# Groups of matmuls added behind the last product of a two-layer decoder trunk

## The chip, the cores and the metric

The kernel runs on one core of a Trainium2 chip. The metric is the device time of one execution in microseconds (us), lower is better; for the kernel before it is the median of two runs. A core has five engines with a queue each: TensorE (PE in the profile, with its weight loads shown apart as PEld), VectorE (DVE), ScalarE (ACT), GpSimd (POOL) and SyncE (SP). They wait for each other through semaphores. A matmul takes a stationary operand (the weights, 128 x 128) and a moving operand (128 partitions by up to 512 columns) from SBUF and writes to a bank of PSUM.

## The reference

The kernel computes a decoder trunk of two layers over 512 tokens with a model width of 1024. Cut to what matters:

```python
def hybrid_layer(x, ...):
    h = rmsnorm(x, g_mix)
    z = h @ w_in                       # one projection, split into nine parts
    ya = sliding_window_sink_attention(aq, ak, av, sinks) @ w_a
    r  = chunkwise_retention(rq, rk, rv)
    yb = (group-normed r * silu(rg)) @ w_b
    x = x + (sigmoid(ga) * ya + sigmoid(gb) * yb) @ w_out
    h2 = rmsnorm(x, g_mlp)
    return x + square(relu(h2 @ w_up)) @ w_down

def reference(x, ...):
    for l in range(2):
        x = hybrid_layer(x, ...)
    return rmsnorm(x, g_final)
```

## The kernel before

Activations lie with the width on the partitions: eight tiles of 128 by 512 tokens. Every float32 factor is held as a sum of two reduced parts of type float32r, a high and a low one: `xh` and `xl` for the activations, `hi` and `lo` for a unit of weights (1024 columns). A product is three matmuls, high by high, high by low and low by high, all accumulated in one PSUM bank (function `products`, lines 395 to 397; in `by_halves`, line 410, the same three in another order). Matmuls have 512 moving columns in the plain projections and 256 in those parts that work by halves (`pair`, and `output` with its line 1301).

Weights stream from device memory; ScalarE makes `hi` (line 343), VectorE `lo` (line 344). These tiles have 1024 + 64 columns of room. For the units named in `ASIDE = ("pair", "wo")` the weights begin `LINE = 16` elements into the tile, for all others at its start. In the built program `xh`, `xl` and the tiles `hi` and `lo` all begin at the same remainder modulo 256 bytes (64 elements), as do the tiles of activations, so where weights begin can be told by the elements past that place, modulo 64: 0 or 16 in this kernel.

PSUM has eight banks in two pools, `ps_mm` with five and `ps_aux` with three. A new bank of a pool is the one that was used longest ago, and the framework makes its first matmul wait for whoever used it last. The framework also orders each engine's queue. `tc.issue_after(ins)` fixes an order on one engine: what is issued inside comes after `ins`. `latest[0]` holds the last matmul that was issued.

The program ends with the second layer's last block, `down_plain`: the last product (lines 395 to 397 with `mm<-hi,r`, its final tile in two halves of 256 columns, its stationary operand a tile of activations named `r`, which begins at 0), then on VectorE and ScalarE the last normalisation (lines 1656 to 1685), then two stores of `y_out` (lines 1683 and 1686), then a closing in which SyncE waits for every engine and queue.

Some matmuls in the kernel are issued without their result being read: eight at the start (line 375, `warm`), and one at lines 1289 and 1560 each, which write a bank before others accumulate into it.

Of the kernel before, what the change touches and what calls it, by code (L numbers as in the profile page):

```python
# [17 lines left out]
P = 128  # L18
T = 512
# [61 lines left out]
class Slots:  # L81
# [12 lines left out]
    def one(self):  # L94
        part = [f for f in self.free if 0 < len(f) < 4]
        f = min(part, key=len) if part else next(f for f in self.free if f)
        return f.pop(0)
# [1683 lines left out]
        layer_body(layer)  # L1781

def _by_chunk(w, cols):

    return w[:, cols].reshape(-1, P, len(cols)).transpose(1, 0, 2)
# [158 lines left out]
```

## Time and profile before

| What | us |
|---|---|
| median of 2 runs | 1455.31 (1455.17 to 1455.45) |
| the profiled execution's own time | 1457.31 |
| its span, first to last instruction | 1455.2 |

In the page's rows "busy" is the time in which an engine had an instruction in work; matmuls overlap, so a busy TensorE need not be at its peak. PEclk is the clock that TensorE was granted, in tenths of full speed, for 40 equal slices of the span. The chain that ended last is followed back from the last instruction to what released each step. A row of it has a start, a length and what it was; rows of equal work are merged, with their count behind an x. Timeline rows begin with a start and a duration, too; from the start of one row to the start of the next is the pace, which for matmuls is less than the duration of one.

### The profile page before, as it was taken

Reading aid. Unit: us, or ns where it says so; the run is one execution under the profiler, and the core shown is the slowest. Engines: PE = TensorE matmul, PEld = TensorE weight load, DVE = VectorE, ACT = ScalarE, POOL = GpSimd, SP = SyncE. Lnnn points to the kernel's source line nnn. Section 1 sums busy time; section 2 is a strip of 40 time slices with the busy share of each in tenths; the row PEclk is TensorE's granted clock in tenths of the full one; section 3 lists DMA queues with packets and bytes.
Section 4 is the critical chain, followed back from the end, with each engine's and each line's share of the span. In section 5 each row is a group of like instructions: output and inputs, shape, how many; then the busy total and the mean of one; then the engine's idle time right before and its main releaser. Section 6 shows DMA issues by size and latency. Waiting matters only on the chain.

```text
span 1455.2 us, 22150 instructions
## 1 busy us (share of the span) xinstructions
PE 1443.0 (99%) x8041; PEld 1258.8 (87%) x8041; DVE 1167.0 (80%) x1762; ACT 969.2 (67%) x1592; POOL 222.6 (15%) x329
## 2 busy tenths in 40 slices
PE   9999999999999999999999999999999999999998
PEld 7888888888988999999888888888889799999997
DVE  6978876866998888888778788687778988787885
ACT  6657555543687777777756575565437877777775
POOL 0011012112101111112201110112120011111120
PEclk9999999999999999999999999999999999999999
DMA  7598359799745677666955983797875477777664
GB/s 258 177 290 225 105 165 303 237 247 248 232 124 196 191 200 186 175 182 179 310 177 170 295 222 108 215 293 223 221 214 175 138 202 199 195 193 197 177 188 149
DMA packets 96428, 297.57 MB, mean 204 GB/s; under 512 B 11328, under 2 KB 11456, under 8 KB 90432
## 3 DMA queue, kind: packets, MB, share of 16 engines
q0 software_dynamic: 35936, 125.58, 37.2%
q1 hardware_dynamic: 59664, 169.27, 33.5%
q8 instruction: 63, 1.03, 0.3%
q10 hardware_dynamic: 720, 1.31, 0.2%
q14 instruction: 45, 0.37, 0.1%
HBM read 256.54 MB, written 115.87 MB: 256 GB/s over the span
## 4 chain that ended last, share of the span: by engine, by line
PE 94%; DMA 2%; ACT 2%; DVE 1%; issue 1%; SPq 0%; DVEq 0%; ACTq 0%
PE mm L395 23%; PE mm L396 23%; PE mm L397 22%; PE wo L1301 5%; PE b L395 2%; PE b L396 2%; PE b L397 2%; PE rv L396 2%; PE rv L395 2%; PE rv L397 2%; PE mm L410 2%; DMA raw<-w_pair_in 1%; PE score L778 1%; PE pT L743 1%; PE r L397 1%; PE r L396 1%
## 5 line engine op out<-in xcount | busy, mean ns | idle before, releaser
L343 ACT ACTIVATE hi<-raw 128x1024 fp32r<-128x1024 f32 (+1 forms) x387 | 394.3, 1021 | 257.5 <-PE mm L396 137.1
L344 DVE TENSOR_TENSOR lo<-raw,hi 128x1024 fp32r<-128x1024 f32 (+1 forms) x388 | 452.3, 1173 | 105.8 <-ACT hi L343 104.4
L395 PE MATMUL mm<-xh,hi 128*128 128x512 f32 (+1 forms) x976 | 343.1, 355 | 1.6 <-ACT xh L418 0.9
L396 PE MATMUL mm<-xl,hi 128*128 128x512 f32 (+1 forms) x976 | 343.6, 355 | 0.0
L397 PE MATMUL mm<-xh,lo 128*128 128x512 f32 (+1 forms) x976 | 339.5, 354 | 0.0
L395 PEld LDWEIGHTS mm<-xh,hi 128*128 128x128 f32 x976 | 183.9, 189 | 27.6 <-ACT xh L418 1.6
L396 PEld LDWEIGHTS mm<-xl,hi 128*128 128x128 f32 x976 | 185.0, 190 | 24.2
L397 PEld LDWEIGHTS mm<-xh,lo 128*128 128x128 f32 x976 | 182.7, 188 | 23.6
L397 PE MATMUL mm<-r,lo 128*128 128x256 f32 (+1 forms) x608 | 187.9, 309 | 0.0
L396 PE MATMUL mm<-r,hi 128*128 128x256 f32 (+1 forms) x608 | 187.9, 309 | 0.0
L395 PE MATMUL mm<-r,hi 128*128 128x256 f32 (+1 forms) x608 | 185.6, 309 | 0.5 <-ACT mm L1476 0.5
L395 PEld LDWEIGHTS mm<-r,hi 128*128 128x128 f32 x608 | 114.7, 189 | 8.5 <-ACT mm L1476 0.7
L396 PEld LDWEIGHTS mm<-r,hi 128*128 128x128 f32 x608 | 115.2, 189 | 7.8
L397 PEld LDWEIGHTS mm<-r,lo 128*128 128x128 f32 x608 | 114.1, 188 | 6.2
L1624 POOL DMA_DIRECT2D y<-eu x56 | 62.3, 1351 | 370.8 <-DVE eu L1609 370.2
L396 PE MATMUL mm<-lo,r 128*128 128x512 f32 (+1 forms) x276 | 104.6, 388 | 0.0
L397 PE MATMUL mm<-hi,r 128*128 128x512 f32 (+1 forms) x276 | 101.3, 387 | 0.0
L395 PE MATMUL mm<-hi,r 128*128 128x512 f32 (+1 forms) x276 | 98.4, 390 | 0.9 <-ACT eu L1619 0.6
L395 PE MATMUL b<-hi,r 128*128 128x512 f32 x180 | 70.5, 392 | 1.6 <-DVE eu L1609 1.2
L396 PE MATMUL b<-lo,r 128*128 128x512 f32 x180 | 70.3, 390 | 0.0
L1301 PE MATMUL wo<-r,hi 128*128 128x256 f32 x384 | 68.0, 281 | 0.0
L397 PE MATMUL b<-hi,r 128*128 128x512 f32 x180 | 67.9, 390 | 0.0
(323 smaller groups left out, 2679.5 us busy)
## 6 DMA issues: line engine op xcount, KB each, us to landing
raw<-w_in_in SPq DMA_DIRECT2D x73, 512.0 KB, 5.9
sums_down<-w_down_in POOLq DMA_DIRECT2D x30, 1024.0 KB, 11.6
sums_up<-w_pair_in POOLq DMA_DIRECT2D x56, 512.0 KB, 10.5
raw<-w_down_in SPq DMA_DIRECT2D x45, 512.0 KB, 7.8
raw<-w_pair_in SPq DMA_DIRECT2D x84, 256.0 KB, 3.7
y<-y POOLq DMA_DIRECT2D x63, 256.0 KB, 9.2
y<-eu POOLq DMA_DIRECT2D x61, 256.0 KB, 8.0
raw<-sums_down SPq DMA_DIRECT2D x30, 512.0 KB, 7.3
```

The source lines that it names most:

```text
L343: state["high"] = nc.scalar.activation(hi[:, at], raw[:, at], AF.Copy).ins
L344: nc.vector.tensor_tensor(lo[:, at], raw[:, at], f32(hi[:, at]), ALU.subtract)
L395: nc.tensor.matmul(ps, ah, bh, start=start and i == 0, stop=False, **more)
L396: nc.tensor.matmul(ps, ah, bl, start=False, stop=False, **more)
L397: latest[0] = nc.tensor.matmul(ps, al, bh, start=False, stop=stop and i == n - 1, **more).ins
L410: latest[0] = nc.tensor.matmul(ps, w[:, cols(j, c)], moving[k][low], start=first, stop=bool(final)).ins
L743: nc.tensor.transpose(pt[:, i * P : (i + 1) * P], sm[:, at : at + P], ident)
L778: nc.tensor.matmul(ps[:, g * w : (g + 1) * w], q_s[g][:, c, at], part[:, keys], start=i == 0, stop=i == 1)
L1301: latest[0] = nc.tensor.matmul(o, w[:, cols], v, start=start and first and n % 2 == 0 and w is hi and v is vh, stop=final and w is lo, ski ...
L1624: nc.gpsimd.dma_start(y[:, 2 * j + m, i * T : (i + 1) * T], t, **how)
```

## The change

A function `paces` is added at the end of the program and called behind both layers. It takes groups of matmuls from one helper, `run(n, ats, count, moving)`: a new bank of `ps_aux`, then `count` matmuls of `n` moving columns, each with start and stop set. The moving operand is the beginning of `xh`, the stationary one 128 columns of `xl` that begin `at` elements in. Where `ats` has several values they take turns. Each matmul is tied behind the one before. Nobody reads the banks; the output does not depend on them.

- 32 groups of 15, first of 512, then of 256 columns, with starts in turn `a, a, b` for `a` and `b` out of 0, 16, 32, 48
- 8 groups of 10 of 512 columns whose moving operand is written as 2, 4, 8 or 32 pieces that adjoin (in the built program they are one run of 512 columns), starts 0 and 48
- 9 groups of 10 with a moving operand of two pieces of 256 columns with 16, 32 or 48 elements between them, starts 0, 16 and 48
- 4 groups of 10 of 512 columns with starts 60, 62, 6 and 10
- then triples and quadruples: 10 matmuls of 512 columns at start 0, a short group of 1 to 6 of 256 or 512, then 12 (or 8) of 256 at start 16 or 48; at the end 4 of 128 columns and 12 of 256

That makes 638 matmuls of 512 columns, 466 of 256 and 4 of 128, in 105 groups.

TensorE's queue at the end of the program (a minus stands for the kernel before, a plus for the one after; the names are output and operands, `r_85` is the tile of activations that the last product reads; L1941 and L1996 are the program's end):

```order
 L396 MATMUL mm<-lo,r_85 128x256
 L397 MATMUL mm<-hi,r_85 128x256
-L1941 UNCONDITIONAL_BRANCH
+L1793 MATMUL pace<-xh,xl 128x512 x240
+L1793 MATMUL pace<-xh,xl 128x256 x240
+L1793 MATMUL pace<-xh,xl 128x512 x220
+L1793 MATMUL pace<-xh,xl 128x256 x13
+L1793 MATMUL pace<-xh,xl 128x512 x10
```

Nothing ahead of this place is moved, on TensorE or on another engine; the added work stands between the last product and the program's end.

The beginning of the added rows with the waits shown (PE_49 is TensorE's own semaphore):

```order
 L396 MATMUL mm<-lo,r_85 128x256
 L397 MATMUL mm<-hi,r_85 128x256
-L1941 UNCONDITIONAL_BRANCH
+L1793 MATMUL pace<-xh,xl 128x512 x45
+L1793 MATMUL pace<-xh,xl 128x512 [waits PE_49]
+L1793 MATMUL pace<-xh,xl 128x512 x14
+L1793 MATMUL pace<-xh,xl 128x512 [waits PE_49]
+L1793 MATMUL pace<-xh,xl 128x512 x14
```

The first three groups wait for nothing; from then on the first matmul of each group waits for the end of the group that used its bank before, three groups back (102 such waits).

```diff
+    def paces():
+        mv, st = (t.rearrange("p k t -> p (k t)") for t in (xh, xl))
+
+        def bank_for(n):
+            return bank(ps_aux, "pace")[:, :n]
+
+        def one(ps, n, at, moving=None):
+            with tc.issue_after(latest[0]):
+                b = mv[:, :n] if moving is None else moving
+                latest[0] = nc.tensor.matmul(ps, st[:, at : at + P], b, start=True, stop=True).ins
+
+        def run(n, ats, count, moving=None):
+            ps = bank_for(n)
+            for i in range(count):
+                one(ps, n, ats[i % len(ats)], moving)
+
+        W, N = T, P * 2
+        for n in (W, N):
+            for a in range(0, 64, 16):
+                for b in range(0, 64, 16):
+                    run(n, (a, a, b), 15)
+        for c in (2, 4, 8, 32):
+            for at in (0, 48):
+                run(W, (at,), 10, mv[:, :W].rearrange("p (a b) -> p a b", a=c))
+        for gap in (16, 32, 48):
+            for at in (0, 16, 48):
+                two = mv[:, : 2 * (N + gap)].rearrange("p (a b) -> p a b", a=2)[:, :, :N]
+                run(W, (at,), 10, two)
+        for at in (60, 62, 6, 10):
+            run(W, (at,), 10)
+        for n in (1, 2, 3, 4, 6):
+            run(W, (0,), 10)
+            run(N, (0,), n)
+            run(N, (48,), 12)
+        for n in (1, 2, 3):
+            for at in (16, 48):
+                run(W, (0,), 10)
+                run(W, (16,), n)
+                run(N, (at,), 12)
+        for n in (1, 2, 3):
+            run(W, (0,), 10)
+            run(N, (0,), n)
+            run(N, (16,), 12)
+        for at in (16, 48):
+            run(W, (0,), 10)
+            run(N, (0,), 4)
+            run(N, (48,), 8)
+            run(W, (at,), 8)
+        run(P, (0,), 4)
+        run(N, (48,), 12)
+
+    paces()
```

## The prediction

> **What bounds the kernel now.** I read the page's busy shares and clock first, then the chain that ended last, then that chain and the timeline row by row where the change attaches: behind the last product.
>
> ```profile
> PE 1443.0 (99%) x8041; PEld 1258.8 (87%) x8041; DVE 1167.0 (80%) x1762; ACT 969.2 (67%) x1592; POOL 222.6 (15%) x329
> PEclk9999999999999999999999999999999999999999
> PE 94%; DMA 2%; ACT 2%; DVE 1%; issue 1%; SPq 0%; DVEq 0%; ACTq 0%
> ```
>
> TensorE is the bound: it is busy 99% of the span and carries 94% of the chain that ended last, at full clock in every slice. Whatever is queued on it behind the last product adds to the end, apart from what fits beside the kernel's tail. That tail comes next, from the chain (start, length, what) and from the timeline.
>
> ```profile
> 1448.68 0.12 PE mm L396
> 1448.80 0.13 PE mm L397
> 1448.93 0.02 issue
> 1448.95 0.48 DVE x L1656
> ...
> 1450.61 0.75 DVE x L1682
> ```
>
> ```profile
> 1451.39 0.33 SPq L1683 DMA_DIRECT2D y_out<-x  x1
> DMA to landing us min/median/max: 2.0/2.4/2.8
> ```
>
> The last product finishes at 1448.93 us. VectorE and ScalarE finish the last rows of the output, their store is issued at 1451.39, lands by 1451.39 + 2.8 = 1454.19 at the latest, and the program ends at its span, 1455.24. So 6.31 us lie between the last product and the end, and at least 1455.24 - 1454.19 = 1.05 us of that is the closing of the program, which waits for every engine. The other 5.26 us can run beside added matmuls.
>
> **The parts of the change.** It removes and moves nothing: on the other four engines the rows stay the same, and the new work stands on TensorE alone. By the loops it is 638 matmuls of 512 columns, 466 of 256 and 4 of 128, 1108 in all, in 105 groups, each with a weight load of its own. No DMA is issued and no other engine waits for the results.
>
> *First: do they begin at once?* They read xh and xl, written long before, and write banks of a pool whose last readers were done earlier. From the fourth group on, a group's first matmul waits for the group three before it, the last user of its bank. At least eleven matmuls lie between, so that is satisfied long before it is asked. The trace holds such a case: line 1560 issues a lone matmul with start and stop into a rotated bank, and its wait is for TensorE itself.
>
> ```profile
> 470.05 0.39 PE L397 MATMUL mm<-hi,r 128*128 128x512 f32 x1
> 470.28 0.39 PE L1560 MATMUL b<-xh,ones 128*128 128x512 f32 x1
> 470.51 0.62 PE L395 MATMUL mm<-hi,r 128*128 128x512 f32 x2
> ```
>
> It starts 0.23 us after the one ahead and the next 0.23 us after it, as without a wait. I cost the 102 waits at nothing; what covers them is the two groups in between, at least 1.3 us of work (11 x 0.12 us).
>
> *Second: the pace of 512 columns.* Only the distance from start to start counts, not the 0.39 us that one lasts, since they overlap. A run of the chain gives it.
>
> ```profile
> 741.65 8.39 PE mm L410 x37
> 1432.79 0.98 PE L395 MATMUL mm<-hi,r 128*128 128x512 f32 x3
> 1433.61 0.86 PE L396 MATMUL mm<-lo,r 128*128 128x512 f32 x3
> 1434.30 0.86 PE L397 MATMUL mm<-hi,r 128*128 128x512 f32 x3
> 1434.99 0.40 PE L395 MATMUL mm<-hi,r 128*128 128x512 f32 x1
> 1435.23 0.39 PE L396 MATMUL mm<-lo,r 128*128 128x512 f32 x1
> 1435.46 0.39 PE L397 MATMUL mm<-hi,r 128*128 128x512 f32 x1
> 1435.68 0.39 PE L395 MATMUL mm<-hi,r 128*128 128x512 f32 x1
> ```
>
> Settled, 8.39/37 = 0.2268 us each. After a stall (the second row) the next come slower: rows of three that last 0.86 have (0.86 - 0.39)/2 = 0.235 us between starts, and after some six the distance is 0.23 and 0.22 again. So a disturbed sequence loses about 6 x 0.008 = 0.05 us before it settles. The change goes from a short group back to 512 columns about 19 times: 1.0 us. Term: 638 x 0.2268 + 1.0 = 145.7 us. Ends: 144.7 with no such loss, 638 x 0.235 = 149.9 if they never settle, which the mixed groups (two loads from one place, one from another) could do.
>
> *Third: the pace of 256 columns.* Here the trace has several values, by where the weights begin. For line 1301 the tiles hi and lo are placed 16 elements in; in the last products the weights begin at 0.
>
> ```profile
> 365.69 32.13 PE wo L1301 x273
> 1086.05 33.92 PE wo L1301 x288
> 1120.85 5.46 PE wo L1301 x48
> 1445.88 0.28 PE L395 MATMUL mm<-hi,r 128*128 128x256 f32 x1
> 1448.28 0.28 PE L397 MATMUL mm<-hi,r 128*128 128x256 f32 x1
> 240.78 0.28 PE L396 MATMUL r<-late,r 128*128 128x256 f32 x1
> 240.90 0.29 PE L397 MATMUL r<-late,r 128*128 128x256 f32 x1
> 241.03 0.22 PE L395 MATMUL r<-r,r 128*128 128x128 f32 x1
> 241.08 0.28 PE L396 MATMUL r<-late,r 128*128 128x128 f32 x1
> 241.20 0.27 PE L397 MATMUL r<-r,r 128*128 128x128 f32 x1
> 241.31 0.44 PE L396 MATMUL mm<-xl,hi 128*128 128x512 f32 x1
> ```
>
> 32.13/273 = 0.1177 and 33.92/288 = 0.1178 us at start 16; 5.46/48 = 0.1138 in a later run of the same line, so one place can hold two paces; (1448.28 - 1445.88)/20 = 0.120 at start 0; 0.13 (240.90 to 241.03) in a change of sizes. Starts 32 and 48, which 244 of the 466 matmuls use, occur nowhere in the trace. They lie among these for all that the rows tell: I take 0.118, the value of the two long runs, and keep 0.1138 and 0.127 as ends. Term: 466 x 0.118 = 55.0 us (53.0 to 59.2). The four of 128 columns: their starts lie 0.05, 0.12 and 0.11 apart, so 0.45 us in all, 0.2 at the least.
>
> *Fourth: moving operand in pieces, and starts off 16.* The pieces that adjoin (2, 4, 8, 32 of them) are one run of 512 in the built program, so they cost what 512 costs. The 90 matmuls with a gap between two halves, and the 40 whose weights begin at 60, 62, 6 or 10, have no like in the trace; both lie inside the ends of the second term, and I take its middle value, because their weight load (0.19 us, next row) has room beside 0.2268.
>
> ```profile
> L1301 PEld LDWEIGHTS wo<-r,hi x384: 187/188/192, 365.3 to 1125.8; 128*128 128x128 f32 x192
> ```
>
> *Sum.* 145.7 + 55.0 + 0.45 = 201.2 us more TensorE work, of which 5.26 lie beside the tail: 195.9. The end by the rows: 1448.93 + 201.2 + 1.05 = 1651.2, against the span of 1455.24. The profiled execution's own time was 1457.31, 2.0 above the median of the runs (1455.31); the difference is added to the median: 1455.31 + 195.9 = 1651.2 us. The ends: 144.7 + 53.0 + 0.2 = 197.9 gives 1647.9; 149.9 + 59.2 + 0.45 = 209.6 gives 1659.6.
>
> The rows speak against one rule of the Trainium skill. Its page "TensorE: Matmul & The Clock Gate", section "Back-to-back issue gap", puts the warm distance of single matmuls at N / 2.4 + 2.5 ns, that is 216 ns for 512 columns and 109 ns for 256. By it the added work would be an estimated 138 + 51 = 189 us and the time about 1639. This trace has 0.2268 and 0.1138 to 0.120 us for those sizes at full clock, and no run of equal matmuls reaches that rule, so the sum goes by the rows.
>
> **The rivals.**
> - *Weights at 32 or 48 are slow to load.* If reading weights from there keeps a 256-column matmul waiting for its load, the distance is the load's 0.19 us instead of 0.118: 244 x 0.071 = 17.3 us more, 1668.5. Groups of 512 hide a load of 0.19 either way. For it: start 0 costs 2 ns more than 16, so places matter. Against: that is all that two places differ by.
> - *New starts are faster than any in the trace.* From start 0 to 16 the best row saves 0.120 - 0.1138 = 0.0062 us for 256 columns. If another place takes that off once more, and twice as much from 512 columns, it is 638 x 0.2144 + 466 x 0.1076 + 0.45 = 187.4 us and 1637.4. Against: 0.2268 is twice 0.1134, so the best rows of both sizes already stand at one rate per column. The Trainium skill's rule above comes out near this time.
> - *Each group's wait empties the pipeline.* Then the next start waits for the end, 0.39 instead of 0.227: 102 x 0.163 = 16.6 us, 1667.8. Against it are the rows of line 1560.
> - *Not slower: the matmuls are not run.* Nobody reads the results, and if they are dropped on the way to the chip the time stays at 1455. This needs all but 5.26 us of the 201 to go before it decides. Against it stand eight matmuls of line 375, whose result nobody reads either, all in the trace, each with its load:
>
> ```profile
> L375 PEld LDWEIGHTS warm<-ones x8: 287/330/333, 1.1 to 3.8; 128*128 128x128 f32 x8
> L375 PE MATMUL warm<-ones x8: 628/628/794, 1.1 to 4.2; 128*128 128x512 f32 x8
> ```
>
> **How the numbers follow.** The forecast has 0.86, slow loads 0.06, new starts that are faster 0.04, emptied pipelines 0.03, not run 0.01. The range takes the ends 1647.9 and 1659.6 and some 1.5 us on either side for what one execution differs from a median: 1646 to 1661; that leaves out the rivals, 0.14. All cases but the last are slower by over 2% (about what a measurement of this kernel can tell from no change): 0.99; within 2%: 0.01; faster: no case, 0.0.
>
> **What would show it.** Busy TensorE right up to 1 us before the end, 1108 more matmul records, and in the chain a stretch of line 1793 of about 201 us, with 512-column groups at 0.227 and 256-column groups between 0.114 and 0.127. Store and tail should end inside that stretch. A gap of over 0.3 us at group starts would speak for the emptied pipeline; groups at 0.19 for the slow load; 512-column groups under 0.22 for the faster start. The prediction is wrong if a start that the trace does not hold has a pace outside those ends.

## The result and the profile after

| | us |
|---|---|
| before, median of 2 runs | 1455.31 |
| after, median of 2 runs | 1653.17 (1651.68 and 1654.66) |
| ratio | 1.136, interval 1.131 to 1.141 |
| forecast | 1651.2 (1646 to 1661) |
| span of the profiled execution | 1649.7 (before 1455.2) |

All times and ratios below leave out a single slow execution, one of four of the kernel with the low parts at 48, which took 8270 us instead of some 1448 for a reason that is not known.

The page of the changed kernel: busy shares, VectorE's slices, and the chain that ended last.

```profile
PE 1642.7 (100%) x9149; PEld 1432.3 (87%) x9149; DVE 1167.1 (71%) x1762; ACT 968.5 (59%) x1592; POOL 222.2 (13%) x329
DVE  7888779779888888796878786798888888600000
PE 98%; ACT 1%; DVE 0%; DMA 0%; issue 0%; DVEq 0%
```

TensorE has 1108 instructions and 199.7 us more; VectorE has the same 1762 instructions and the same busy time, and its last five slices are empty. The same chain in order of time, at its end, and the last store:

```profile
1446.42 0.12 PE mm L397
1446.54 202.18 PE pace L1793 x1108
```

```profile
1449.01 0.33 SPq L1683 DMA_DIRECT2D y_out<-x  x1
DMA to landing us min/median/max: 2.0/2.4/2.8
```

The last product ends at 1446.54 (2.4 us earlier than in the execution profiled before). From there one unbroken piece of 202.18 us reaches 1648.72, and 0.98 us later the program ends. The store is issued 2.5 us after the last product, as before (1451.39 - 1448.93 = 2.46), and lands beside the added work. So the balance of the two spans closes: 202.2 added, 6.31 - 0.98 = 5.33 covered, 2.4 from the earlier end of the product, 202.2 - 5.3 - 2.4 = 194.5 = 1649.7 - 1455.2.

The added matmuls by form (the two figures behind the bar are busy time in us and the mean length of one in ns), and three stretches of the chain, for the groups in turns of 512 columns, those of 256, and the next 21 groups of 512 (those with pieces and those with odd starts):

```profile
L1793 PE MATMUL pace<-xh,xl 128*128 128x512 f32 x638 | 150.2, 393 | 0.0
L1793 PE MATMUL pace<-xh,xl 128*128 128x256 f32 x466 | 57.4, 280 | 0.0
L1793 PE MATMUL pace<-xh,xl 128*128 128x128 f32 x4 | 0.6, 261 | 0.0
```

```profile
1446.54 55.31 PE pace L1793 x239
1501.85 28.25 PE pace L1793 x239
1530.22 48.38 PE pace L1793 x210
```

The counts are as forecast, and no idle time stands ahead of any of them. The busy times overlap between forms and can't serve as paces. The chain can: 55.31/239 = 0.2314 us for 512 columns, 28.25/239 = 0.1182 for 256, 48.38/210 = 0.2304 for the later groups of 512. From start to start, worked out from the trace's starts over all groups, 512 columns took 147.3 us (0.2309 each), 256 columns 54.5 (0.1169), 128 columns 0.39.

Means of the 32 first groups in ns, from start to start; weights start twice at `a` (the row), then once at `b` (the column):

```
512 columns     b=0    b=16   b=32   b=48     256 columns     b=0    b=16   b=32   b=48
a=0            228.5  230.7  232.1  231.1     a=0            120.0  118.8  119.1  117.7
a=16           231.5  232.8  231.1  231.9     a=16           117.3  117.8  118.2  115.0
a=32           232.5  230.1  232.3  232.9     a=32           117.9  118.0  118.7  117.3
a=48           228.7  232.9  233.8  229.7     a=48           118.1  115.1  117.1  117.7
```

The first group holds the way in; later groups at 0 alone repeat 227, 226, 227. No other place and no turn settles so low with 512 columns. With 256 it is the other way round: 0 alone is the slowest, and two turns stand out, 16, 16, 48 and 48, 48, 16. Their first four or five are slower, then they stay at 113 and 114.

### The profile page after: what moved, and what is told of

Its sections match the earlier page's. It is cut to its first block, busy times and chain, and to the rows that moved or that the text cites. A ratio compares the mean times of both kernels' runs of the same rounds, so it can differ in the third digit from the quotient of the medians.

```text
span 1649.7 us, 24366 instructions
## 1 busy us (share of the span) xinstructions
PE 1642.7 (100%) x9149; PEld 1432.3 (87%) x9149; DVE 1167.1 (71%) x1762; ACT 968.5 (59%) x1592; POOL 222.2 (13%) x329
## 4 chain that ended last, share of the span: by engine, by line
PE 98%; ACT 1%; DVE 0%; DMA 0%; issue 0%; DVEq 0%
PE mm L395 21%; PE mm L397 21%; PE mm L396 21%; PE pace L1793 12%; PE wo L1301 5%; PE b L395 2%; PE b L396 2%; PE b L397 2%; PE rv L395 2%; PE rv L397 2%; PE rv L396 2%; PE mm L410 1%; PE score L778 1%; PE pT L743 1%; PE r L397 1%; PE r L396 1%
## 5 line engine op out<-in xcount | busy, mean ns | idle before, releaser
L1793 PE MATMUL pace<-xh,xl 128*128 128x512 f32 (+1 forms) x1108 | 202.3, 345 | 0.0
L1793 PEld LDWEIGHTS pace<-xh,xl 128*128 128x128 f32 x1108 | 174.8, 188 | 27.4
L395 PE MATMUL b<-hi,r 128*128 128x512 f32 x180 | 70.5, 392 | 1.6 <-DVE eu L1609 1.2
## 6 DMA issues: line engine op xcount, KB each, us to landing
sums_up<-w_pair_in POOLq DMA_DIRECT2D x56, 512.0 KB, 10.5
```

The costliest lines, as they stand in the source:

```text
L395: nc.tensor.matmul(ps, ah, bh, start=start and i == 0, stop=False, **more)
L1793: latest[0] = nc.tensor.matmul(ps, st[:, at : at + P], b, start=True, stop=True).ins
```

## The experiments

**All starts at 0.** The same groups, but every matmul takes its weights from start 0.

```diff
-                one(ps, n, ats[i % len(ats)], moving)
+                one(ps, n, 0, moving)
```

> Every added matmul takes its weights from start 0; group sizes, banks, waits and moving pieces stay. Theory (what keeps the 512-column groups off 226.7 ns is where weights begin and the turns between places): the mixed 512-column groups, 230.7 to 233.8 ns each in the changed kernel, settle at 226.7 to 227.5, so the first 240 take 54.4 to 54.7 us instead of 55.5; the 256-column groups all stand at 119 to 120 ns, none at 113.3 beyond the first two of a group; all 1108 take about 201.5 us. Rival (the extra comes from group starts, that is new banks and waits): the 512-column groups keep 230 ns and more.

The chain of this kernel in the same stretches; then, with another cut, the groups with two pieces, three of the groups that had odd starts, and the whole:

```profile
1446.31 54.20 PE pace L1793 x239
1502.41 26.88 PE pace L1793 x224
1547.92 19.24 PE pace L1793 x83
1570.83 6.35 PE pace L1793 x28
1446.31 201.81 PE pace L1793 x1108
```

512 columns now take 54.20/239 = 0.2268 instead of 0.2314, 256 columns 26.88/224 = 0.1200, in that stretch each of them 120 ns. So places and turns made these 512-column groups slower, not group starts, whose banks and waits are all still there. Over the whole, 512 columns lose 147.3 - 145.6 = 1.7 us to the starts and 256 columns gain 55.8 - 54.5 = 1.3. The total is 0.3 us above what was expected. Moving operands in two pieces have a price of their own here: 19.24/83 = 0.2318 at start 0, where an unbroken operand takes 6.35/28 = 0.2268. Over 90 matmuls that is 0.45 us, enough to account for it.

**One bank.** All groups write one bank, and the 102 waits are gone.

```diff
+        only = bank(ps_aux, "pace")
+
         def bank_for(n):
-            return bank(ps_aux, "pace")[:, :n]
+            return only[:, :n]
```

> All groups write one bank, so the 102 waits are gone; sizes and starts stay. Theory (a wait that is long satisfied costs nothing): the added stretch takes 202.2 us within 0.3, and group by group the paces are those of the changed kernel within 1 ns. Rival (each new bank with its wait costs tens of ns or disturbs the pace): the stretch is 2 us or more shorter, and the groups begin without their slower first matmuls.

```profile
1446.09 202.18 PE pace L1795 x1108
```

The stretch has the same 202.18 us; in no group does the mean distance differ by more than 1 ns, and the sums of all distances, 202.07 us, differ by 1 ns. A wait that is long satisfied costs nothing, and the sequence of paces is the same again in another execution of another program: it goes with the sequence of matmuls and not with chance.

**Forty matmuls.** Only 40 matmuls of 256 columns at start 0 are added.

```diff
-        W, N = T, P * 2
...
+        N = P * 2
+        run(N, (0,), 40)
```

> Only 40 matmuls of 256 columns at start 0 are added, 4.8 us of TensorE work. Theory (the tail of 5.26 us covers it): TensorE ends about 1 us before the store has landed and the time is that of the kernel before within 0.5 us. Rival (nothing is covered, or TensorE's work slows the tail): 2 to 5 us more, and VectorE's or ScalarE's last instructions are longer than 0.75 us or begin later than before.

```profile
1446.30 4.80 PE pace L1793 x40
```

```profile
1448.77 0.33 SPq L1683 DMA_DIRECT2D y_out<-x  x1
```

TensorE is done at 1451.10; the store is issued at 1448.77, 2.47 us after the last product, and with the longest landing of 2.8 us, which the prediction took, it is down by 1451.57, 0.5 us later than TensorE (about 1 us was expected). This execution's span is 1452.6, so the end comes 3.8 us after the store's issue, as before (1455.24 - 1451.39 = 3.85). The time is 1456.15 against 1456.74 beside it, ratio 1.000 (0.9991 to 1.001). So 4.8 us of matmuls are covered by the tail and don't slow it.

**Both operands 16 further on.** Moving operand and weights are both taken 16 elements later.

```diff
-                b = mv[:, :n] if moving is None else moving
-                latest[0] = nc.tensor.matmul(ps, st[:, at : at + P], b, start=True, stop=True).ins
+                b = mv[:, 16 : 16 + n] if moving is None else moving
+                latest[0] = nc.tensor.matmul(ps, st[:, 16 + at : 16 + at + P], b, start=True, stop=True).ins
...
-                run(W, (at,), 10, mv[:, :W].rearrange("p (a b) -> p a b", a=c))
+                run(W, (at,), 10, mv[:, 16 : 16 + W].rearrange("p (a b) -> p a b", a=c))
...
-                two = mv[:, : 2 * (N + gap)].rearrange("p (a b) -> p a b", a=2)[:, :, :N]
+                two = mv[:, 16 : 16 + 2 * (N + gap)].rearrange("p (a b) -> p a b", a=2)[:, :, :N]
```

> Every added matmul takes its moving operand and its weights from 16 elements further on, so the distance between the two stays. Theory (only the distance of the two starts modulo 64 elements matters): group by group the paces are those of the changed kernel within 1 ns, the stretch 202.2 us within 0.3. Rival (the place of the weights itself matters, whatever the moving operand does): groups at 0 now behave as those at 16 did, 512 columns at 232.8 ns instead of 226.7 and 256 columns at 117.8 instead of 120.

```profile
1447.77 202.20 PE pace L1793 x1108
```

202.20 us, and every group but the first stands within 1 ns of the changed kernel. The first comes from the last product, which was not moved, and takes 229.7 instead of 228.5. For this shift, the one that was tried, what counts is the distance between the start of the weights and that of the moving operand, not where either lies. That the distance counts modulo 64 elements was taken from the layout and has no test of its own here.

**The way in.** The same 12 matmuls at 48 had two paces in the changed kernel. Behind 10 of 512 columns and two of 256 at start 0, and then behind three:

```profile
1584.99 1.42 PE pace L1793 x12
1589.07 1.25 PE pace L1793 x11
```

1.42/12 = 0.118 and 1.25/11 = 0.114. The next kernel asks for this alone, behind the last product:

```diff
+        for ats in ((16,), (48,), (16, 16, 48), (48, 48, 16)):
+            for n in range(9):
+                run(W, (0,), 12)
+                if n:
+                    run(N, (0,), n)
+                run(N, ats, 24)
```

> Other groups behind the last product: 12 matmuls of 512 columns at 0, then 0 to 8 of 256 at 0, then 24 of 256 at 16, at 48, or in turns 16, 16, 48 or 48, 48, 16. Theory (at one place the pace has two stable values and the way in picks one, taking turns leaves only the fast one): the 24 at 16 or 48 alone stand at 113.3 ns for some of the nine ways in and at 117.7 for others, each to the end; those in turns reach 113.3 from every way in within about eight. Rival (the place or the turns fix the pace and the way in only delays it): each of the four has one value at the end of its 24. Length by the counts: 36 x (12 x 0.2268 + 24 x 0.116) + 144 x 0.12 = 215 us.

The chain, cut to single groups: at 16, at 48, and in the turns 16, 16, 48, each behind one and behind two matmuls at 0 (the turns only behind two); then the turns 48, 48, 16 behind two and behind three.

```profile
1455.09 2.61 PE pace L1793 x23
1460.79 2.71 PE pace L1793 x23
...
1509.39 2.61 PE pace L1793 x23
1515.09 2.71 PE pace L1793 x23
...
1568.59 2.63 PE pace L1793 x23
...
1622.28 2.73 PE pace L1793 x23
1628.25 2.50 PE pace L1793 x22
```

2.61/23 = 0.1135 and 2.71/23 = 0.1178: two paces at one place, each kept to the end of its 24. All 36 ways in, by their distances from start to start:

```
behind n at 0:      0     1     2     3     4     5     6     7     8
16               117.8 113.3 117.8 117.9 117.9 117.9 117.9 117.9 117.9
48               117.7 113.3 117.7 113.3 113.3 113.3 113.3 113.3 113.3
16, 16, 48       114.2 113.3 114.2 114.0 114.0 114.0 114.0 114.0 114.0
48, 48, 16       113.7 113.3 118.8 113.3 113.3 113.3 113.3 113.3 113.3
```

The theory holds for 16 and 48 alone, and for 16, 16, 48, which is at 113 or 114 by its sixth matmul from every way in (the means above 114 hold those first five). It falls for 48, 48, 16: behind two it stays at 118.8 (2.73/23 = 0.1187), so these turns have a slow way as well. The length, 215.21 us, is the 215 that was expected.

**Turns in the kernel itself.** The kernel's own products of 256 columns take high, high, low in `products` and at line 1301, with both parts 16 aside. This version has no added groups and sets the low part 48 aside:

```diff
-                wpool.tile([P, UNIT + 4 * LINE], F32R, tag=n, name=n, bufs=SPLIT + 1)[:, aside : aside + UNIT]
-                for n in ("hi", "lo")
+                wpool.tile([P, UNIT + 4 * LINE], F32R, tag=n, name=n, bufs=SPLIT + 1)[:, at : at + UNIT]
+                for n, at in (("hi", aside), ("lo", 3 * aside))
```

> The kernel before, without the added groups; the low parts of the weights that are set 16 elements aside are set 48 aside instead, the high parts stay at 16, so the sequence of starts in these 256-column products becomes 16, 16, 48. Theory (pace is set by the turns between places alone, as the added group with 16, 16, 48 showed, 113.3 ns settled against 117.8 at 16 alone): some 3000 matmuls of 256 columns fall from 117.8 to about 113.5 ns, 13 us less, about 1442. Rival (in the kernel other things disturb the lock, or VectorE and ScalarE, which feed TensorE, take up what it saves): below 3 us, 1452 to 1456.

```profile
PE 1433.8 (99%) x8041; PEld 1248.1 (86%) x8041; DVE 1165.9 (81%) x1762; ACT 969.7 (67%) x1592; POOL 223.6 (15%) x329
1081.75 32.67 PE wo L1301 x288
1115.29 5.50 PE wo L1301 x48
```

The run at line 1301 that took 33.92 us takes 32.67, 0.1134 each. Over some 3020 distances behind a 256-column matmul with weights set aside (a few stalls of over 0.4 us left out) the mean falls from 117.8 to 114.3 ns, 10.5 us in all. What is left above 113.3 comes to 3 us: 1.2 from matmuls of 115 to 122 ns, most of them in fours, as at the beginning of the added groups in these turns, and the rest from longer breaks. The ratio is 0.9938 (0.9921 to 0.9954), some 9 us: less than the 13 expected, which counted neither ways in nor the some 250 of these distances that stood at 113 or 114 in the kernel before already, and well above the rival's 3.

**The other way round, and both at 48.** With high 48 and low 16:

```diff
+                for n, at in (("hi", 3 * aside), ("lo", aside))
```

> As the kernel with the low parts at 48, but the other way round: high parts 48 aside, low parts 16, so the starts take turns 48, 48, 16. Theory (taking turns between 16 and 48 locks the pace whichever comes twice, as the added groups 16, 16, 48 and 48, 48, 16 both did): 256-column products at about 114 ns, 9 to 11 us less than before. Rival (it needs the low part at 48): 117 ns or more and under 3 us less.

```profile
1079.67 32.65 PE wo L1301 x288
1113.20 5.71 PE wo L1301 x48
```

The gain in time is the same within the intervals: ratio 0.994 (0.9925 to 0.9955), mean 114.5 ns. But the slow way that these turns showed behind two matmuls occurs in the kernel too: the later run at line 1301 stands at 5.71/48 = 0.119, where high 16 and low 48 had 5.50/48 = 0.115. So of the two orders 16, 16, 48 is the one for which no slow way was seen. With both parts at 48 there is no turn:

```diff
+                for n, at in (("hi", 3 * aside), ("lo", 3 * aside))
```

> High and low parts both 48 aside, no turns. Theory (it is the turns, not the place 48, that gave 114 ns): the 256-column products stand at about 117.7 ns as in the kernel before, the time within 2 us of it. Rival (48 is the better place): about 114 ns and 9 us less.

```profile
1084.34 33.92 PE wo L1301 x288
```

33.92 us, as before; mean 117.8 ns, ratio 0.9995 (0.9986 to 1.0005). So it is the turn that gives the gain, not the place 48, although 48 alone had the fast pace for seven ways in of nine: in the kernel nearly all of its distances stand on the slow pace, only some 130 of 3020 at 113 or 114. Which of the matmuls ahead bring that about was not traced.

**The faster version once more.** High part at 16, low part at 48, in more executions.

> The same kernel as the one with the high parts at 16 and the low parts at 48, once more and in more rounds, for the size of the gain. Theory (TensorE's 10.5 us shorter 256-column products reach the end nearly whole): 8 to 10 us less than the kernel before, a ratio of 0.993 to 0.9945 with an interval that leaves out 1. Rival (the first interval was luck of few executions): a ratio above 0.997.

1447.24 us against 1456.54, ratio 0.994 (0.9927 to 0.9954), and again 32.67 us for that run:

```profile
1081.20 32.67 PE wo L1301 x288
```

This version beats the kernel before by 0.6%; both of its intervals leave out 1.

## Why the prediction was right

- **The work stands bare behind the last product, but for the tail.** Right: one piece of 202.18 us in the chain, 5.33 us covered (5.26 forecast), closing 0.98 (1.05). Forty matmuls alone cost nothing, which shows the cover by itself.
- **Waits at nothing.** Right, shown by the kernel with one bank.
- **512 columns, 145.7 us.** Measured 147.3. The base of 0.2268 holds for weights at start 0: it is what all starts at 0 gave. Wrong was that the term let groups at every place and in every turn settle there. Places other than 0 and turns have means of 229 to 234 ns, near the upper end of the term (0.235, groups that never settle), which I had kept for the range only; that is the 1.7 us which the starts add. The 1.0 us on top for coming back from short groups was twice too much: with all starts at 0 the sum is 145.6, 0.9 above 638 x 0.2268, and of that the pieces are 0.45. So the sign that I named, 512-column groups at 0.227, came for start 0 alone.
- **256 columns, 55.0 us.** Measured 54.5, inside the ends. The middle value of 0.118 holds for most groups, and the fast value of 0.1138, which I kept as an end, is the mean of a run on a second steady pace of 113.3 with its first matmuls. Starts 32 and 48 lay among the known values, as taken, but six groups at 48 settle at 113.3, half a ns under that end: by the letter of the prediction's last sentence this speaks against it, though the pace itself stood in the kernel before already, at start 16.
- **Pieces and odd starts.** Adjoining pieces are one run. The 90 matmuls with a gap cost 0.232 where the term had about 0.228, which is 0.3 us of its 1.6; the 40 at 60, 62, 6 and 10 had means of 230 to 233 ns, so 0.2268 was too low for them, too. The four of 128 columns took 0.39 instead of 0.45.
- **The sum** was 201.2, measured 202.2. It is nearer than its largest term by some luck: the 0.5 us too much for 256 columns makes up for a third of the 1.6 too little for 512. The median lies 2.0 us above the forecast; 1.0 is this, and the rest lies within what executions differ by: the two of the changed kernel are 3.0 us apart, and the kernel before ran from 1454.4 to 1457.5 beside the last experiment.
- **The rivals.** No group is near 0.19 us (slow load), none settles under 226 ns for 512 or 113 for 256 columns (new starts that are faster), nothing is emptied at group starts, and all 1108 ran. The rule of the Trainium skill's page "TensorE: Matmul & The Clock Gate", section "Back-to-back issue gap", 216 and 109 ns, is met by no settled group here: the lowest are 226.7 and 113.3 at full clock.

## What to carry to other kernels

Cost a run of equal matmuls by the distance of their starts in a run of the chain, not by their lengths, and take only the tail behind the last one off. Where pace depends on where operands begin, look for two steady values in one profile (here 33.92/288 and 5.46/48 us at one line): the lower one shows what the same code can do, and a small change of layout may keep it there, as turns did here (0.6% of the kernel's time). Test such a change on groups behind the kernel's end first, with several ways in, then in the kernel, with the place alone as a control.

## What was not expected of the hardware

- A float32r matmul of 256 columns whose weights begin 16 or 48 elements past the moving operand's place has two steady paces, 113.3 and 117.8 ns, and the matmuls ahead pick one: behind one matmul of 256 columns at start 0 both places have the fast one, behind none or two the slow one. With all weights at the moving operand's own place a run of them settled at 120 in every group. Why there are two was not settled; that each sequence repeats within 1 ns speaks against chance.
- Weights in turns 16, 16, 48 end at 113.3 from all nine ways in that were tried, 48, 48, 16 from eight, and the slow way of the latter occurs in the kernel as well.
- 226.7 ns for 512 columns and 113.3 for 256 are one rate, 0.443 ns per column, and nothing went below it once settled.
- With weights at start 0, a moving operand of 512 columns in two pieces costs 3 to 7 ns more than an unbroken one (means of groups from 229.9 with 48 elements between the pieces to 233.3 with 16, in the kernel with all starts at 0, against 226.7). With weights at 16 the changed kernel shows no such price: 231.7 to 233.5 in two pieces, 232.8 unbroken.
